# Five halves of expert weights loaded ahead of the overflow branch instead of ten, and the context's first split behind the copies of x

## The chip, the cores and the metric

The kernel runs on one core of a Trainium2 chip. The metric is the device time of one execution in microseconds (us). A core has a matrix engine (PE, with its weight loads as PEld), a vector engine (DVE), a scalar engine (ACT), a general engine (POOL) and an engine for synchronisation (SP), which in this kernel issues nearly all loads. Each engine runs its own list of instructions in order and waits for the others by semaphores.

## The reference, cut to what matters

The network has two blocks. The first mixes 256 tokens of width 1024, adds the result to x and then adds a mixture of experts: a router gives each token two of 32 experts, and each expert is a gated feed-forward network with a hidden width of 512. The second block needs keys and values of a 256-token context, which depend on the context alone and can be computed at any time.

```python
x = x + gt1 * mix
h2 = modulate(rms_norm(x, norm2_g[layer]), sh2, sc2)
x = x + gt2 * moe_ffn(h2.reshape(-1, D_MODEL), *moe_args).reshape(x.shape)
...
def moe_ffn(u, rg_w, rg_b, re_w, re_b, w1, w3, w2):
    ...
    yb = (jax.nn.silu(xblk @ w1[e]) * (xblk @ w3[e])) @ w2[e]
...
pc = modulate_2(rms_norm_2(cx, norm1_g[l]), csh1, csc1) @ w_in[l]
```

## The kernel before, in words

**Tiles.** Tokens are held as two halves of 128 partitions. All sums are in f32; a weight of a large product is split by `split_w` (L277) into a high part `wh` (ACT, L206) and a low part `wl` = `w` - `wh` (DVE, L209), and PE makes three products (`hh` by `wh`, `hl` by `wh`, `hh` by `wl`) where there was one. Splits come from a pool of 5 buffers. Weights come in halves of 128 x 2048 f32, 1 MB each, by `half` (L243) from the SP queue; in the expert stage ten buffers hold them.

**The place of the change.** At the end of the first mixer, `residual_part` adds the mixer's last product to x, in two halves of 512 columns. `route_part` (L911) transposes each finished piece of x on PE (products of `ident` by `x`), copies the result to `xT` on ACT and DVE by turns (L915, L916) and multiplies it by the router's weights on PE (into `pm_527`). `route_rows` (L921) scales these into `logit` on DVE. `route` (L929) is a chain of some 30 small DVE operations: the best group, the two best experts in it, `cnt`, then two kinds of small products on PE (`pm_591`), then `pos`, the place of each token in its expert's list, and `maxcnt` (L982), the largest number of tokens of one expert.

**Side steps.** `route_all` (L1077) also calls `side(SIDE0)` with `SIDE0` = 2: two steps of the context's computation, which is spread as filler over the expert stage, one step for each expert. The first two steps here are the products of the context with three chunks of `w_in_2`, of which the halves `w_603`, `w_604`, `w_615` and `w_616` matter here. `w_603` and `w_604` give 48 products of 128 x 256 each (`pf_605`, `pf_606`), `w_615` and `w_616` give 24 products of 128 x 512 each (`pf_617`, `pf_618`); the results go to `kvc`, which ACT writes to memory as `kv_d` (768 KB).

**The branch.** `overflow` (L1157) reads `maxcnt` into a register of every engine (L1161) and skips a block for lists of more than 32 tokens (L1162). With these inputs the block is never run. All engines pass the branch and wait for each other behind it. Behind it come the experts: `gather` (L1001) builds the one-hot matrix `oh` from `pos` on DVE, PE multiplies it with `xn` (16 products, `pm_718` and `pm_719`, recorded as 32), and ACT and DVE by turns scale the result into `xg`. `expert` then needs six halves of weights: two of e1, two of e3, two of e2. Expert 0 has `w_724` to `w_729`, expert 1 has `w_755` to `w_760`.

**What sets the order.** The program is written in the order of the computation, and the tile framework's scheduler then decides the order of instructions on each engine, by its own simulated times and by the dependences. `self.hold` is a list of pairs of instructions: `split_w` pops one pair and orders the high and the low split behind its two members (`behind`, a dependence of order). Expert 0's and 1's loads, which depend on no computation, were placed ahead of the branch by the scheduler as far as buffers allowed.

Of the kernel before, what the change touches and what calls it, by code (L numbers as in the profile page):

```python
# [20 lines left out]
P = 128  # L21
# [8 lines left out]
BGA = 1.34  # L30
NM = 0
XA, XB = 3, 5
SIDE, SIDE0 = 1.0, 2


C1 = dict(c=0, g1=16, g2=24, qk=32, hyu=40, cw=52, cb=88, skip=100, ffn=104)
# [5 lines left out]
class Lhs:  # L42
    def __init__(self, hi, lo):
        self.hi, self.lo = hi, lo
# [66 lines left out]
class Builder:  # L111
    def __init__(self, tc, a, ctx):
        self.tc, self.nc, self.a, self.ctx = tc, tc.nc, a, ctx
        E = ctx.enter_context
        self.p16 = E(tc.tile_pool(name="p16", bufs=5))
        self.p16x, self.nchunk = None, 0
        self.pspx, self.nsp = None, 0
        self.psp = E(tc.tile_pool(name="psp", bufs=5))
        self.p0 = E(tc.tile_pool(name="p0", bufs=1))
        self.psm = E(tc.tile_pool(name="psm", bufs=18))  # L120
        self.pr = E(tc.tile_pool(name="pr", bufs=4))
        self.pa = E(tc.tile_pool(name="pa", bufs=4, space=PSUM))
        self.pm = E(tc.tile_pool(name="pm", bufs=2, space=PSUM))
        self.pf = E(tc.tile_pool(name="pf", bufs=2, space=PSUM))
        self.n = 0
        self.p1 = None
        self.fill = False
        self.bg = None
        self.rot = 0
        self.flow = ""  # L130
        self.hold, self.gap = [], None
        self.early, self.s8 = (), None
        self.misc_pools, self.lin_misc = ["m"], False

# [87 lines left out]
        return self.nc.vector.scalar_tensor_tensor(out, a, s, b, op0=op0, op1=op1)  # L222

    def load(self, t, src):
        self.nc.sync.dma_start(t, src)

    def lsm(self, t, src):
        self.nc.gpsimd.dma_start(t, src)
# [14 lines left out]
    def half(self, src):  # L243
        self.nchunk += 1
        x = self.p16x and self.nchunk * self.nx % (5 + self.nx) < self.nx
        pool = self.p16x if x else self.p16
        t = pool.tile([P, 2048], F32, tag="T16", name=self.nm("w"))
        self.load(t, src)
        return t


# [659 lines left out]
    def route_part(self, x, xT, p, i):  # L911

        for k in range(4 * i, 4 * i + 4, 2):
            q = self.tr_pair(x, k)
            self.act(xT[:, k, :], q[:, 0, :])  # L915
            self.nc.vector.tensor_copy(xT[:, k + 1, :], q[:, 1, :])  # L916
            for kk in range(k, k + 2):
                for t in range(2):
                    self.mm(p[:, t], xT[:, kk, t * P:(t + 1) * P], self.router[0][:, kk, :], t == 0 and kk == 0, kk == 7)
# [81 lines left out]
    def gather(self, xn, A, B, e0, n):  # L1001

        oh = self.t2([P, 2, 8, 32], F32, "oh")[:, :, :n]
        es = slice(e0, e0 + n)
        for t in range(2):
            self.tt(oh[:, t], self.iota.unsqueeze(1).to_broadcast([P, n, 32]),
                    self.pos[:, t, es].unsqueeze(2).to_broadcast([P, n, 32]), ALU.is_equal)
        xg = self.t8([P, 8, 256], F32, "xg")
        w = 32 * n
        per = 512 // w  # L1010
        for d0 in range(0, 8, per):
            p = self.ps().rearrange("p (i s) -> p i s", s=w)
            for i, t in itertools.product(range(per), range(2)):
                d = d0 + i
                self.mm(p[:, i], xn[:, t, d * P:(d + 1) * P], oh[:, t].rearrange("p e c -> p (e c)"),
                        i == 0 and t == 0, t == 1)
            for i in range(per):
                d = d0 + i
                if i % 2 == 0:
                    self.act(xg[:, d, :w], p[:, i], AF.Identity, scale=A[:, d:d + 1], bias=B[:, d:d + 1])  # L1020
                else:
                    self.ts(xg[:, d, :w], p[:, i], A[:, d:d + 1], B[:, d:d + 1], ALU.mult, ALU.add)
        return oh, xg
# [53 lines left out]
    def route_all(self, x, side, more):  # L1077

        self.p_keep = self.p1
        xn = self.t8([P, 2, 1024], F32, "xn")  # L1080
        with self.tc.tile_pool(name="over", bufs=1) as self.p1:
            self.route()
            for t in range(2):
                self.ts(xn[:, t, :], x[:, t, :], self.r2[:, t:t + 1])
            side(SIDE0)
            for _ in range(NM):
                next(more)
            self.overflow(x, xn)
        return xn, self.A2, self.B2
# [872 lines left out]
def _tables():  # L1962
# [17 lines left out]
    def rope(half, nf):  # L1980
        inv = (f(10000.0) ** (-np.arange(nf, dtype=f) / f(nf))).astype(f)
        ang = np.zeros((2 * half, 256), f)
        rot = np.zeros((2 * half, 2 * half), f)
        for s, pos in ((0, r), (1, c)):
            for i in range(nf):
                a, b = s * half + i, s * half + nf + i
                ang[a] = ang[b] = pos * inv[i]
                rot[b, a] = -1.0
                rot[a, b] = 1.0
        return np.cos(ang), np.sin(ang), rot  # L1990
# [118 lines left out]
```

## Time and profile before

| what | value |
|---|---|
| median of 3 runs | 1779.25 us (1779.24 to 1780.82) |
| the profiled execution's own time | 1783.12 us |
| its span in the profile | 1781.4 us |
| mean granted clock of PE | 0.977 of full speed |
| PE busy | 1673.6 us, 94% of the span |
| DVE, ACT busy | 963.9 us (54%), 727.3 us (41%) |

The span is the profiled execution from its first to its last instruction. The profiled execution took 1783.12 us, 3.87 us more than the median. Times below, such as "at 448.1", are microseconds from the span's start.

### The profile page before, as it was taken

How to read it: one execution, taken by the hardware profiler on the slowest of the kernel's cores; microseconds unless marked ns; L12 is line 12 of the kernel's file. 1: busy time of each engine (PE TensorE's matmuls, PEld its weight loads, DVE VectorE, ACT ScalarE, POOL GpSimd, SP SyncE). 2: the span in 40 equal slices, each digit the busy share in tenths (PEclk: the TensorE clock that was granted, in tenths of full speed). 3: DMA queues.
4: the chain of work that ended last, by engine and by line, in shares of the span. 5: the costliest groups of instructions: out<-in, count | busy, mean ns of one | idle time of the engine just before them, and what ended most of it. 6: DMA issues, size and time to landing. Idle time of an engine off the chain costs nothing.

```text
span 1781.4 us, 31112 instructions
## 1 busy us (share of the span) xinstructions
PE 1673.6 (94%) x12928; PEld 1319.8 (74%) x12928; DVE 963.9 (54%) x1719; ACT 727.3 (41%) x1257; POOL 63.0 (4%) x104
## 2 busy tenths in 40 slices
PE   5999999999798889999999988999999999989998
PEld 1678766668565556777687667868999997689998
DVE  5626556466223445545454466685545466756555
ACT  2414433343223333333333236564444455645443
POOL 0000000000000000000000001010000000100000
PEclk9899999999899999999999999999999999989999
DMA  9654588977699999889999997634867746235551
GB/s 373 274 213 166 206 309 316 349 269 275 245 420 421 420 384 393 351 356 420 420 368 421 420 393 239 205 104 145 292 252 265 269 164 197 81 122 190 190 190 44
DMA packets 79059, 495.82 MB, mean 278 GB/s; under 512 B 8928, under 2 KB 15744, under 8 KB 22464
## 3 DMA queue, kind: packets, MB, share of 16 engines
q1 hardware_dynamic: 74496, 478.30, 69.9%
q0 software_dynamic: 3152, 10.47, 2.1%
q10 hardware_dynamic: 1264, 4.98, 0.7%
q8 instruction: 104, 1.70, 0.4%
q14 instruction: 43, 0.35, 0.1%
HBM read 486.91 MB, written 6.82 MB: 277 GB/s over the span
## 4 chain that ended last, share of the span: by engine, by line
PE 65%; DVE 4%; ACT 3%; issue 2%; DMA 1%; DVEq 0%; ACTq 0%
PE pf L200 24%; PE pm L200 19%; PE acc L200 11%; PE pa L200 5%; PE pj L200 2%; PE pm L203 1%; DMA w<-in_e 1%; PE pf L203 1%; PE pada L200 1%; DVE wl L209 1%; ACT e L206 0%; DVE sm L1337 0%; DMA w<-in_w_out 0%; ACT wh L206 0%; ACT eh L206 0%
## 5 line engine op out<-in xcount | busy, mean ns | idle before, releaser
L209 DVE TENSOR_TENSOR wl<-w,wh 128x1024 fp32r<-128x1024 f32 x346 | 422.2, 1224 | 399.1 <-PE pa L200 105.0
L206 ACT ACTIVATE wh<-w 128x1024 fp32r<-128x1024 f32 x346 | 362.5, 1057 | 406.2 <-PE pa L200 169.4
L200 PE MATMUL pf<-hh,wh 128*128 128x256 f32 x592 | 167.0, 284 | 3.6 <-ACT hh L206 2.3
L200 PE MATMUL pf<-hl,wh 128*128 128x256 f32 x592 | 165.5, 281 | 0.6 <-DVE hl L209 0.6
L200 PE MATMUL pf<-hh,wl 128*128 128x256 f32 x592 | 164.0, 282 | 1.5 <-DVE wl L209 1.5
L200 PE MATMUL acc<-hh,wh 128*128 128x256 f32 x512 | 143.5, 280 | 0.0
L200 PE MATMUL acc<-hl,wh 128*128 128x256 f32 x512 | 142.9, 279 | 0.0
L200 PE MATMUL acc<-hh,wl 128*128 128x256 f32 x512 | 142.8, 279 | 0.0
L200 PE MATMUL pm<-w,xg 128*32 128x256 f32 x2048 | 133.2, 392 | 2.5 <-DMA w<-in_e 1.2
L200 PEld LDWEIGHTS pf<-hh,wh 128*128 128x128 f32 x592 | 111.8, 189 | 8.6 <-issue 3.3
L200 PEld LDWEIGHTS pf<-hl,wh 128*128 128x128 f32 x592 | 111.8, 189 | 2.6 <-issue 1.2
L200 PEld LDWEIGHTS pf<-hh,wl 128*128 128x128 f32 x592 | 110.6, 189 | 3.4 <-DVE wl L209 2.5
L200 PEld LDWEIGHTS pm<-w,xg 128*32 128x32 f32 x2048 | 67.0, 112 | 52.3 <-issue 14.3
L200 PEld LDWEIGHTS acc<-hh,wh 128*128 128x128 f32 x512 | 96.4, 188 | 5.9 <-ACT wh L206 4.2
L200 PEld LDWEIGHTS acc<-hh,wl 128*128 128x128 f32 x512 | 96.7, 189 | 0.0
L200 PEld LDWEIGHTS acc<-hl,wh 128*128 128x128 f32 x512 | 96.4, 188 | 0.0
L200 PE MATMUL pada<-w,csil 128*32 128x512 f32 x576 | 84.5, 620 | 4.3 <-DMA w<-in_ada_w 4.3
L200 PE MATMUL pm<-w,ex 128*32 128x256 f32 x1024 | 62.1, 382 | 16.7 <-issue 15.5
L200 PE MATMUL pm<-hl,wh 128*128 128x256 f32 x256 | 71.7, 280 | 0.0
L200 PE MATMUL pm<-hh,wh 128*128 128x256 f32 x256 | 71.7, 280 | 0.0
L200 PE MATMUL pm<-hh,wl 128*128 128x256 f32 x256 | 71.4, 279 | 0.0
L200 PE MATMUL pf<-wl,hh 128*128 128x512 f32 x160 | 65.3, 408 | 0.0
(512 smaller groups left out, 3473.8 us busy)
## 6 DMA issues: line engine op xcount, KB each, us to landing
w<-in_e SPq DMA_DIRECT2D x192, 1024.0 KB, 12.4
w<-in_ff SPq DMA_DIRECT2D x96, 1024.0 KB, 5.0
w<-in_ada_w SPq DMA_DIRECT2D x72, 1024.0 KB, 7.0
w<-in_w_in SPq DMA_DIRECT2D x54, 1024.0 KB, 7.3
w<-in_w_out SPq DMA_DIRECT2D x16, 1024.0 KB, 7.1
w<-in_ret_w_o SPq DMA_DIRECT2D x4, 1024.0 KB, 5.3
w<-in_w_su SPq DMA_DIRECT2D x3, 1024.0 KB, 4.9
adab<-in_ada_b SPq DMA_DIRECT2D x9, 256.0 KB, 12.6
```

What stands on the lines that cost most here:

```text
L200: return self.nc.tensor.matmul(out, lhsT, rhs, start=start, stop=stop, skip_group_check=True)
L203: return self.nc.tensor.transpose(out, in_, self.ident)
L206: return self.nc.scalar.activation(out, in_, f, **k)
L209: return self.nc.vector.tensor_tensor(out, a, b, op=op)
```

## The change

The change has two parts. `gather` keeps the second of its first two `oh` operations as `self.gate`; from then on `half` counts its loads and gives numbers 6 to 15 a dependence on it, with a semaphore. The scheduler may thus put five halves (`w_724` to `w_728`) ahead of the branch and no more. And `route_all` fills `hold` with the last two copies into `xT`, so that the next `split_w`, which is that of the first half of `w_603`, is ordered behind them.

```diff
-SIDE, SIDE0 = 1.0, 2
+SIDE, SIDE0, EARLY = 1.0, 2, 5
...
+        self.gate, self.loads = None, 0
...
     def load(self, t, src):
-        self.nc.sync.dma_start(t, src)
+        return self.nc.sync.dma_start(t, src)
...
-        self.load(t, src)
+        i = self.load(t, src)
+        if self.gate:
+            self.loads += 1
+            if EARLY < self.loads <= EARLY + 10:
+                self.tc.add_manual_dep(i.ins, self.gate.ins.name, mybir.DependencyInfo(mybir.DependencyClass.Sync,
+                                       mybir.DependencyReason.DATA), reason="behind the branch")
         return t
...
-            self.act(xT[:, k, :], q[:, 0, :])
-            self.nc.vector.tensor_copy(xT[:, k + 1, :], q[:, 1, :])
+            self.moved = self.act(xT[:, k, :], q[:, 0, :]), self.nc.vector.tensor_copy(xT[:, k + 1, :], q[:, 1, :])
...
-            self.tt(oh[:, t], self.iota.unsqueeze(1).to_broadcast([P, n, 32]),
+            i = self.tt(oh[:, t], self.iota.unsqueeze(1).to_broadcast([P, n, 32]),
                     self.pos[:, t, es].unsqueeze(2).to_broadcast([P, n, 32]), ALU.is_equal)
+        self.gate = self.gate or i
...
             for t in range(2):
                 self.ts(xn[:, t, :], x[:, t, :], self.r2[:, t:t + 1])
+            self.hold = [self.moved]
             side(SIDE0)
```

Three engines' orders show it. First SP, whose instructions are the loads; `maxcnt` is its read of the register for the branch. Before, the last loads ahead of the branch:

```order
L225 DMA w_755_4072<-in_e1 128x2048
L225 DMA w_604_3283<-in_w_in_2 128x2048
L225 DMA w_616_3406<-in_w_in_2 128x2048
L225 DMA w_725_3938<-in_e3 128x2048
L225 DMA w_727_3942<-in_e3 128x2048
L225 DMA w_729_3946<-in_e2 128x2048
L225 DMA w_756_4074<-in_e3 128x2048
L225 DMA w_757_4076<-in_e1 128x2048
L225 DMA w_758_4078<-in_e3 128x2048
L1161 TENSOR_LOAD maxcnt_3251
```

And in the change, where line numbers are larger by 1 to 7:

```order
L226 DMA w_604_3283<-in_w_in_2 128x2048
L226 DMA w_616_3406<-in_w_in_2 128x2048
L226 DMA w_725_3938<-in_e3 128x2048
L226 DMA w_727_3942<-in_e3 128x2048
L1168 TENSOR_LOAD maxcnt_3251
...
L1169 UNCONDITIONAL_BRANCH
L226 DMA w_729_3946<-in_e2 128x2048
L226 DMA w_755_4072<-in_e1 128x2048
L226 DMA w_756_4074<-in_e3 128x2048
L226 DMA w_757_4076<-in_e1 128x2048
L226 DMA w_758_4078<-in_e3 128x2048
```

Five halves, `w_729` and `w_755` to `w_758`, moved from before the branch to right behind it.

Second DVE, around the chain of the router from `logit` on. Before, three low splits stand ahead of `logit` here (and those of `w_603` further up):

```order
L209 TENSOR_TENSOR wl_612_3344<-w_604_3283,wh_611_3343 128x1024
L916 COPY xT_526_2893<-pm_566_3124 128x256
L209 TENSOR_TENSOR wl_614_3372<-w_604_3283,wh_613_3371 128x1024
L209 TENSOR_TENSOR wl_620_3411<-w_615_3404,wh_619_3410 128x1024
L222 SCALAR_TENSOR_TENSOR logit_575_3157<-pm_527_2894,r2_567_3135,router_2879 128x36 x2
L933 TENSOR_REDUCE sm_577_3203<-logit_575_3157 128x2
...
L209 TENSOR_TENSOR pr_580_3211<-logit_575_3157,sm_578_3205 128x64
L209 TENSOR_TENSOR wl_622_3427<-w_615_3404,wh_621_3426 128x1024
L933 TENSOR_REDUCE sm_581_3213<-pr_580_3211 128x16
```

And in the change:

```order
L921 COPY xT_526_2893<-pm_566_3124 128x256
L210 TENSOR_TENSOR wl_608_3288<-w_603_3281,wh_607_3287 128x1024
L210 TENSOR_TENSOR wl_610_3316<-w_603_3281,wh_609_3315 128x1024
L223 SCALAR_TENSOR_TENSOR logit_575_3157<-pm_527_2894,r2_567_3135,router_2879 128x36 x2
L938 TENSOR_REDUCE sm_577_3203<-logit_575_3157 128x2
...
L210 TENSOR_TENSOR cnt_3235<-sm_578_3205,sm_589_3233 128x64
L210 TENSOR_TENSOR wl_614_3372<-w_604_3283,wh_613_3371 128x1024
L223 SCALAR_TENSOR_TENSOR pos_3246<-pm_591_3240,cnt_3235 128x64
```

The two low splits of `w_603` come behind the last copy into `xT`, `logit` comes right behind them, and the splits of `w_604` come within the chain. The low splits of `w_616` (`wl_624`, `wl_626`) stand behind the branch and behind `oh`.

Third PE, at the branch. Before, all products of `w_616` (splits `wh_623` to `wl_626`) and the first score product of the context, `pf_739`, precede the branch, and the gather follows it:

```order
L200 MATMUL pf_618_3409<-wh_625_3458,hh_505_2818 128x512
L200 MATMUL pf_618_3409<-wl_626_3459,hh_505_2818 128x512
L200 MATMUL pf_618_3409<-wh_625_3458,hl_506_2819 128x512
L200 MATMUL pf_739_4030<-kvc_495_2793,pad_601_3277 128x256
L1161 TENSOR_LOAD maxcnt_3251
...
L200 MATMUL pm_718_3899<-oh_716_3895,xn_576_3197 128x128 x7
L200 MATMUL pm_719_3912<-oh_716_3895,xn_576_3197 128x128 x7
```

And in the change:

```order
L201 MATMUL pf_618_3409<-wh_621_3426,hl_506_2819 128x512
L1168 TENSOR_LOAD maxcnt_3251
...
L201 MATMUL pf_617_3408<-wh_623_3442,hh_505_2818 128x512
L201 MATMUL pf_618_3409<-wh_623_3442,hh_505_2818 128x512
L201 MATMUL pm_718_3899<-oh_716_3895,xn_576_3197 128x128 x6
L201 MATMUL pf_617_3408<-wl_624_3443,hh_505_2818 128x512
...
L201 MATMUL pf_618_3409<-wh_625_3458,hl_506_2819 128x512
L201 MATMUL pm_718_3899<-oh_716_3895,xn_576_3197 128x128
L201 MATMUL pm_719_3912<-oh_716_3895,xn_576_3197 128x128 x8
L201 MATMUL pf_739_4030<-kvc_495_2793,pad_601_3277 128x256
```

All 24 products of `w_616` and `pf_739` moved behind the branch, where they stand among the products of the gather. Behind it on ACT are now also the high split `wh_625`, the four copies into `kvc`, which stand ahead of the first `xg`, and the write of `kv_d`. Ahead of the branch, PE has the router's transposes and products in one run and the products of `w_603` behind them, where before these began first and the router's stood among them. The scheduler's order also differs in details of the expert stage up to about a half of PE's list, and nowhere after that.

## Rows read from the trace of the kernel before

**Rows 1.** The page's busy time of each engine, and its chain that ended last.

```profile
PE 1673.6 (94%) x12928; PEld 1319.8 (74%) x12928; DVE 963.9 (54%) x1719; ACT 727.3 (41%) x1257; POOL 63.0 (4%) x104
...
PE 65%; DVE 4%; ACT 3%; issue 2%; DMA 1%; DVEq 0%; ACTq 0%
```

**Rows 2.** The chain of waits behind the branch: start us, us, what.

```profile
454.53 6.77 PE pm L200 x32
...
461.33 0.47 ACT xg L206
...
463.11 3.99 PE pm L200 x64
```

**Rows 3.** Instructions of the branch's two lines: ns min/median/max, first and last start.

```profile
L1161 SPq TENSOR_LOAD <-maxcnt x1: 469/469/469, 445.7 to 445.7; - x1
...
L1161 PEldq TENSOR_LOAD <-maxcnt x1: 489/489/489, 448.1 to 448.1; - x1
...
L1162 SPq COMPARE_BRANCH x1: 50/50/50, 446.6 to 446.6; - x1
L1162 PEldq COMPARE_BRANCH x1: 5212/5212/5212, 448.7 to 448.7; - x1
```

**Rows 4.** What SP waited for, 440 to 466 us: total, times, longest us.

```profile
SPq L225 <- PE pm L200: 12.9, 1, 12.9
...
SPq L1161 <- DVE maxcnt L982: 3.2, 1, 3.2
```

**Rows 5.** Timeline of PE ahead of the branch: start us, us, work, idle before it.

```profile
417.09 0.28 PE L200 MATMUL pf<-hh,wh 128*128 128x256 f32 x1
...
426.80 0.38 PE L200 MATMUL pf<-hh,wh 128*128 128x256 f32 x1 [1.33 <-ACT wh L206]
...
434.87 0.50 PE L200 MATMUL pf<-wh,hh 128*128 128x512 f32 x1 [0.99 <-ACT pad L206]
```

**Rows 6.** Timeline of DVE ahead of the branch.

```profile
419.19 0.68 DVE L209 TENSOR_TENSOR x<-x,a 128x512 f32<-128x512 f32 x1
...
426.78 1.23 DVE L209 TENSOR_TENSOR wl<-w,wh 128x1024 fp32r<-128x1024 f32 x1 [1.60 <-ACT wh L206]
...
431.73 0.41 DVE L222 SCALAR_TENSOR_TENSOR logit<-pm,r,router 128x36 f32<-128x36 f32 x2
...
439.79 0.23 DVE L209 TENSOR_TENSOR cnt<-sm,sm 128x64 f32<-128x64 f32 x1
...
445.49 0.15 DVE L982 CAST maxcnt<-sm 128x1 int32<-128x1 f32 x1
```

**Rows 7.** Timeline of ACT ahead of the branch.

```profile
446.79 1.35 ACT L206 ACTIVATE kvc<-pf 128x256 f32<-128x256 f32 x4 [0.57 <-PE pf L200]
```

**Rows 8.** Stretches: us, busy us (instructions) of PE, PEld, DVE, ACT, POOL, PEclk, DMA, GB/s.

```profile
424.00:434.00 10.00, 8.39 (x70) 7.83 (x68) 6.61 (x15) 5.00 (x7) 0.99 (x2) 1.00 1.01 419
...
450.47:454.50 4.03, 0.00 (x0) 0.00 (x0) 0.40 (x2) 0.00 (x0) 0.00 (x0) 0.50 0.13 46
454.50:460.70 6.20, 6.17 (x29) 6.20 (x30) 1.34 (x5) 0.91 (x2) 0.50 (x1) 0.50 0.01 3
...
703.06:706.47 3.41, 1.73 (x33) 0.82 (x25) 3.31 (x12) 2.03 (x4) 0.79 (x1) 1.00 0.95 348
706.47:713.30 6.83, 6.83 (x52) 3.80 (x52) 4.90 (x14) 2.53 (x6) 0.00 (x0) 0.50 0.78 277
```

**Rows 9.** DMA by queue 448 to 450 and 450 to 452 us, and an issue.

```profile
q10 hardware_dynamic: 71, 0.44, 52.8%
...
q8 instruction: 1, 0.02, 3.0%
...
kv_d<-kvc ACTq DMA_DIRECT2D x1, 768.0 KB, 3.9
```

**Rows 10.** Timeline of PE, the second gather.

```profile
505.87 3.62 PE L200 MATMUL pm<-oh,xn 128*128 128x128 f32 x30
```

**Rows 11.** The chain of waits, 640 to 760 us.

```profile
656.38 17.48 DMA w<-in_e
```

## The prediction

> **What bounds the kernel now.** I read the page first. PE is busy 94% of the span, and the chain that ended last runs on PE for 65% of it, with small shares of DVE and ACT and 1% of waits for loads [rows 1]. So a change gains where it closes a hole of PE, and loses where it opens one. The change works between 417 and 467 us; the next view is therefore the chain of waits there. It enters behind the branch: a gather on PE of 6.77 us from 454.53, then `xg` (0.47 us on ACT), then expert 0's products at 463.11 [rows 2]. From there to the end the work follows from expert 0 step by step, mostly on PE, so I take it that a shift of 463.11 arrives at the end undiminished, and make my sum to that time.
>
> Next come the branch's own instructions. SP reads the register at 445.7 and its compare takes 0.05 us. PE arrives last but for DVE and ACT, at 448.1, and its compare takes 5.21 us [rows 3]; the gather begins at 454.53, so the branch costs PE 454.53 - 448.1 = 6.4 us. What does SP wait for there? It waits 3.2 us for `maxcnt` and only behind the branch 12.9 us for buffers, which expert 0's products free [rows 4]. The branch thus waits for PE and the router's chain and not for the expert weights ahead of it. That is the first finding against the edit's plain reading.
>
> Last I read the stretches. PE had nothing to do from its read of the register at 448.1 on; from 450.47 to 460.70 it was granted half of its clock (1.2 of 2.4 GHz), and 6.2 us of that were work [rows 3, 8]. The gather shows the price: 32 recorded products in 6.77 us, against 30 in 3.62 us in the second gather [rows 2, 10].
>
> **Part one, the loads.** Five halves leave the queue ahead of the branch. A half is 128 x 2048 x 4 bytes = 1.05 MB; at the 419 GB/s of a stretch with busy DMA engines it takes 2.5 us [rows 8]. PE's wait of 1.33 us at 426.80, ahead of `w_604`'s first product, has a part that goes away, since `w_755` no longer stands ahead of `w_604` [rows 5]; the second part of the change moves that product anyway. Behind the branch five halves need 5 x 2.5 = 12.4 us. Issued at about 449.3, as `oh` is done, they have landed by about 463.4 (with 1.7 us for a start). Expert 0's first products need `w_724` to `w_727`, which are early; `w_729` is needed with the second half of its output product, about 4.9 us after 463.11, and expert 1's halves later. Behind the waiting loads SP has only later halves, and those waited for expert 0 to free a buffer anyway (12.9 us [rows 4]); POOL has no part in it. Cost: nothing. The cover is the gather and `xg`; without it, two halves' time, 5 us.
>
> **Part two, the split behind the copies.** Before, the products of `w_603` start at 417.09 and fill PE while x gets its last sum (419.19, 0.68 us) [rows 5, 6]. Now they wait. PE's last mixer product ends at 417.25; then the sum ends at 419.9, two rounds of transposes, copies and router products follow, which I put at 2.4 us each (an estimate; they were spread among other work before); the last copy ends at about 424.8, `wl_608` (1.23 us [rows 6]) is there at 426.0. In between PE has the router's products and the first four high products, about 3.7 us, so a hole of about 5 us opens. In return the chain runs early: `logit` moves from 431.73 to about 427.2, `cnt` from 439.79 to 432.9 and `maxcnt` from 445.49 to about 435, since fewer splits stand ahead of them on DVE [rows 6].
>
> PE up to the branch, then: 48 products of `w_603` at 0.117 us (the spacing of the rows behind 417.09) bring it to 431.2; 48 of `w_604` with the small `cnt` products and a wait for `pos` bring it to 438.0; 1.0 us for `pad` as before at 434.87 [rows 5]; 24 of `w_615` at 0.234 us bring it to 444.6. It arrives 3.5 us before 448.1, but the 24 products of `w_616` and `pf_739` (24 x 0.234 + 0.3 = 5.9 us) are still to do. So PE's work stands 2.4 us later.
>
> **The branch.** What will it cost? The nearest rows differ widely: PE's own 6.4 us above, and about 2 us if PE passed as the other engines did (SP from its read at 445.7 to its compare's end at 446.7 is 1 us [rows 3]; I add 1 us for the others' signals). While PE's compare ran, the write of `kv_d` (768 KB, 3.9 us) had half of the DMA engines' time, and one packet of an instruction queue came only at its end [rows 9]. In the change this write is behind the branch. I take 1.8 us off: 4.6 us, with 6.4 and 2.0 as the ends, nearer to the first because it is PE's own row. PE resumes at 444.6 + 4.6 = 449.2.
>
> The Trainium skill ("Runtime: NRT & Kernel Launch", "Instruction fetch mechanics") says that a taken branch whose target is outside the fetched window must wait for a fetch by DMA; the 5.21 us of PE's compare beside SP's 0.05 agree. But its page "DMA: Bandwidth & Descriptors", "Queues, rings and completion order", says that a DMA engine takes turns between queues packet by packet, so that a write in another queue would hardly delay a fetch; by that rule nothing comes off, and the sum below would be +3.8 instead of +2.0.
>
> **Behind the branch.** To the last context product PE now has 24 products of `w_616` (5.6 us) and seven of the gather's 16 at 0.23 us (3.62 us / 30 x 2 records [rows 10]), together 7.2 us at full clock. The clock falls as before, and I keep 6.2 us at half [rows 8], which costs 3.1 us more: 449.2 + 7.2 + 3.1 = 459.4, rounded over the parts. (If the shorter pause spares half of it, 1.6 less; 8 us at half, 0.9 more.) Then, what is not beside PE's work: four copies into `kvc`, which ACT must finish ahead of the first `xg` (1.35 us [rows 7]), eight `xg` by turns on ACT and DVE of 0.45 us (3.6) [rows 2], and two more ACT operations ahead of expert 0, `sc` and one of a context step (0.8, an estimate from the same row): 5.75 us. Before, the first `xg` could start while the gather ran. Expert 0 starts at 465.1 instead of 463.11.
>
> **Sum.** +2.0 us. The profiled execution is 3.9 us above the median of the runs shown; I add the 2.0 to the median: 1779.25 + 2.0 = about 1781. A change of 0.2% is 3.56 us, about what a measurement of this kernel can tell from no change.
>
> **Rivals.**
> - *The branch costs PE 6.4 us as now.* For it: this is the only row of a PE branch here; the write of `kv_d` took only half of the engines. Against: the packet that came late. Expert 0 starts 1.8 us later: +3.8, 1783.
> - *A cheap branch (the other side: faster).* If PE's fetch is delayed by the write alone, or the target is fetched while PE still multiplies, the branch costs 2.0, and the clock hardly falls because PE paused so briefly: 2.0 - 2.6 - 3.1 = -3.7, about 1775.5. It decides if PE's compare is below 1 us. Against it: no PE branch here shows it.
> - *The clock falls in the new hole (slower).* In the stretch 703.06 to 706.47 PE was busy for half of the time, and the 6.83 us behind it ran at half clock [rows 8]. The hole from 417.3 to 426 has PE busy for less than half. If the clock falls, 3.4 us at half cost 1.7 and 6.8 cost 3.4. With 3.4, and the branch between the two prices (+0.9): 1779.25 + 2.0 + 3.4 + 0.9 = 1785.5. The point of decision is the granted clock behind 420.
> - *The new order of the expert stage.* The scheduler moved rows as far as half way through PE's list. A late load there has its price in the chain: 17.48 us at 656 are a load of expert weights that PE waits on [rows 11]. A quarter of that, some 4 us, I leave open either way: about 1775 or 1785 with the +2.0.
> - *The change doesn't do what it says.* If the branch waits for no loads [rows 4], five loads fewer ahead of it change nothing, and only the second part works. That is already in my sum.
>
> **How the numbers follow.** Chances: forecast 0.40; branch at its old price 0.15 (half of it past 0.2%); cheap branch 0.17 (0.14 past 0.2%); the fallen clock 0.10; the expert stage 0.18, half on each side. Faster: 0.14 + 0.09 = 0.23. Slower: 0.08 + 0.10 + 0.09 = 0.27. The rest, 0.50, is within 0.2%. The likeliest case alone reaches from 1778 (clock spared by half, fetch sooner) to 1784 (old price). The range for 8 in 10 reaches below to the cheap branch with a microsecond more, 1774.5, and above to the fallen clock, 1786.5.
>
> **What would show it.** Right: SP's read of the register near 436 to 445, not held by any load; PE's last product ahead of the branch near 444.6 and its compare about 3.4 us; PE idle some 5 us between 417.3 and 426; the first product of expert 0 near 465. Wrong: a compare of under 1 us on PE, a granted clock of half ahead of 440, `w_729` or an expert 1 half as the releaser of a PE wait, or an end that moved by other than the start of expert 0, which would put the cause in the expert stage.

## The result, and the profile after

| | before | changed kernel |
|---|---|---|
| median | 1780.03 us (4 runs, 1779.24 to 1782.19) | 1795.89 us (4 runs, 1795.17 to 1801.24) |
| ratio | | 1.0085 (95% interval 1.0067 to 1.0102) |
| profiled execution | 1783.12 us, span 1781.4 | 1795.42 us, span 1793.7 |

The change makes the kernel some 16 us slower, outside the predicted range of 1774.5 to 1786.5. The page says little: PE's share is 94% as before and the chain's shares have hardly moved [rows 1]. PE's busy time has grown by 10.2 us with the same 12928 products, so the loss does not show as idle time alone.

```profile
PE 1683.8 (94%) x12928; PEld 1321.3 (74%) x12928; DVE 965.1 (54%) x1719; ACT 727.9 (41%) x1257; POOL 61.6 (3%) x104
...
PE 64%; DVE 4%; ACT 3%; DMA 2%; issue 2%; DVEq 0%; ACTq 0%; SPq 0%
```

So I follow the stages. First the branch (the same view as [rows 3], in the changed kernel: ns min/median/max, first and last start):

```profile
L1168 SPq TENSOR_LOAD <-maxcnt x1: 474/474/474, 436.3 to 436.3; - x1
...
L1168 PEldq TENSOR_LOAD <-maxcnt x1: 487/487/487, 442.3 to 442.3; - x1
...
L1169 PEldq COMPARE_BRANCH  x1: 3309/3309/3309, 442.9 to 442.9; - x1
```

SP reads the register 9.4 us earlier, PE 5.8 us earlier, and PE's compare takes 3.31 us instead of 5.21. What SP waits for, as in [rows 4], here from 415 us on:

```profile
SPq L1168 <- DVE maxcnt L987: 13.7, 1, 13.7
...
SPq L226 <- DVE oh L210: 6.4, 1, 6.4
```

SP's read waits for `maxcnt` alone, longer since no load keeps SP busy, and its next load waits 6.4 us for the gate. What does the branch cost PE? The timeline of PE's first product behind it, before and after (the idle time stands in brackets):

```profile
454.53 6.76 PE L200 MATMUL pm<-oh,xn 128*128 128x128 f32 x32 [6.32 <-DVE oh L209]
```

```profile
446.33 0.70 PE L201 MATMUL pf<-wh,hh 128*128 128x512 f32 x2 [0.26 <-PEq L1169]
```

PE's sequencer reads the register while products that it has issued are still to run: 15 of them start behind the read at 442.3, the last at 445.69. So the compare runs beside work, and PE stands idle for 0.26 us. Before, no product was left behind the read, and it stood idle for 6.32 us. Then the chain behind the branch, as in [rows 2] (start us, us, what), and the stretches, as in [rows 8] (us, busy us of PE, PEld, DVE, ACT, POOL, granted clock, DMA share, GB/s):

```profile
446.33 0.70 PE pf L201 x2
447.04 1.34 PE pm L201 x12
...
453.76 2.01 PE pm L201 x18
455.77 0.45 PE pf L201 x2
...
458.84 3.66 PE pm L201 x64
```

```profile
417.20:422.00 4.80, 3.34 (x24) 2.74 (x24) 4.38 (x18) 1.78 (x6) 1.07 (x2) 1.00 0.19 31
422.00:428.80 6.80, 6.28 (x27) 6.02 (x28) 6.36 (x19) 3.34 (x4) 0.99 (x2) 0.50 0.98 405
428.80:441.60 12.80, 11.80 (x95) 11.37 (x95) 8.93 (x33) 6.54 (x11) 0.00 (x0) 1.00 0.38 157
...
446.30:460.00 13.70, 12.62 (x92) 10.29 (x96) 5.86 (x13) 4.79 (x15) 1.17 (x1) 1.00 0.88 316
```

Expert 0 starts at 458.84, which is 4.3 us *earlier* than before [rows 2]. The clock did fall, but in the new hole ahead of the branch (422.0 to 428.8), and behind the branch it stayed full. So the loss of 12.3 us in the span lies behind expert 0, where the change edits no instruction and only its late halves could still be felt. Where? The copy `eh` marks every expert (32 of them: first and last start in one row). Before and after:

```profile
L206 ACT ACTIVATE eh<-pm x32: 363/384/387, 467.1 to 1067.1; 128x256 f32<-128x256 f32 x32
```

```profile
L207 ACT ACTIVATE eh<-pm x32: 365/385/387, 462.5 to 1077.6; 128x256 f32<-128x256 f32 x32
```

Expert 0 is 4.6 us early, expert 31 10.5 us late. What PE waited for between 465 and 1090 us, before and after (engine, line, releaser: total us, times, longest):

```profile
PE pm L200 <- issue: 15.5, 14, 1.8
...
PE pm L203 <- ACT eh L206: 7.6, 16, 0.6
```

```profile
PE pm L201 <- issue: 21.9, 18, 2.8
PE pm L204 <- ACT eh L207: 10.8, 20, 1.3
```

Eighteen pauses instead of fourteen. An expert has two: after its first products PE needs `eh` from ACT before it can transpose it, and after the transposes it needs two small steps of ACT and DVE before the output products. One such expert (number 19, counted from 0), in the chain of the kernel before and of the changed kernel:

```profile
818.91 3.93 PE pm L200 x68
822.84 3.00 PE pf L200 x12
825.84 0.22 PE pm L203 x2
826.05 2.82 PE pf L200 x12
...
828.88 1.93 PE pm L200 x32
```

```profile
819.22 0.39 ACT eh L207
...
819.66 0.45 PE pm L204 x2
820.11 1.04 issue
821.15 1.93 PE pm L201 x32
823.09 3.00 PE pf L201 x12
```

Before, twelve products of the context (`pf`) stand in each pause. Now the expert's three steps stand one behind the other, PE waits through ACT's copy and the 1.04 us, and twelve of the context's products come afterwards. The printed orders show the same: 14 pauses of each kind without a product in them before, 18 of each now.

To place the loss I matched PE's instructions of two traces one by one by the printed orders and summed, by stretch of the kernel before, how much longer each took up to the next one's start:

```
stretch of before, us     417-465   465-790   790-1090
changed kernel               -4.8      +0.3      +16.6
run one                      +0.2      -5.3       +2.3
run two                      -0.2       0.0      +17.1
second split held            -3.9      -5.0       +3.2
```

(The other rows are runs told below. Single profiles differ from each other by some us, since stretches at half clock lie elsewhere in each.)

How much of the 16.6 us are the pauses? From start to start, between 790 and 1090 us, the step from an expert's first products to its transposes took 8.1 us in 9 pauses before and 12.6 us in 13 now, and the step from the transposes to the output products 10.6 us in 8 and 16.2 us in 12. These are 10 us for four experts, 2.5 us each. Some 2 or 3 us are the clock: the kernel before has no half clock in this stretch, the changed kernel 6.8 us, and run one, with the old order and 7.3 us at half clock, is 2.3 us longer there. The rest are smaller waits, some longer and some shorter than before.

### The profile page after: what moved, and what is told of

Its sections match the earlier page's. It is cut to its first block, busy times and chain, and to the rows that moved or that the text cites. A ratio compares the mean times of both kernels' runs of the same rounds, so it can differ in the third digit from the quotient of the medians.

```text
span 1793.7 us, 31114 instructions
## 1 busy us (share of the span) xinstructions
PE 1683.8 (94%) x12928; PEld 1321.3 (74%) x12928; DVE 965.1 (54%) x1719; ACT 727.9 (41%) x1257; POOL 61.6 (3%) x104
## 4 chain that ended last, share of the span: by engine, by line
PE 64%; DVE 4%; ACT 3%; DMA 2%; issue 2%; DVEq 0%; ACTq 0%; SPq 0%
PE pf L201 24%; PE pm L201 19%; PE acc L201 11%; PE pa L201 5%; PE pj L201 2%; PE pm L204 1%; DMA w<-in_w_in 1%; DVE wl L210 1%; PE pf L204 1%; DMA w<-in_e 1%; PE pada L201 1%; ACT wh L207 1%; ACT e L207 0%; ACT eh L207 0%; DVE sm L1344 0%
## 5 line engine op out<-in xcount | busy, mean ns | idle before, releaser
L201 PE MATMUL pm<-w,xg 128*32 128x256 f32 x2048 | 136.9, 389 | 1.3 <-DMA w<-in_e 0.7
L201 PEld LDWEIGHTS pm<-w,ex 128*32 128x32 f32 x1024 | 34.1, 112 | 46.3 <-issue 29.8
## 6 DMA issues: line engine op xcount, KB each, us to landing
adab<-in_ada_b SPq DMA_DIRECT2D x9, 256.0 KB, 12.6
```

What stands on the lines that cost most here:

```text
L201: return self.nc.tensor.matmul(out, lhsT, rhs, start=start, stop=stop, skip_group_check=True)
```

## The experiments

Theory A: the head of the change, up to expert 0, is no loss; the loss is the scheduler's other order of the expert stage, which leaves more pauses unfilled. Theory B: the five halves loaded late starve a stage that moves weights at 420 GB/s. The tool for it is a table that pins an order. It holds, for each of the five engines, the numbers of the instructions in the order wanted (the loads' order on SP too), and adds a dependence of order, without a semaphore, from each to the one behind it:

```diff
+def pin_order(tc, nc):
+    for ids in ORDER.values():
+        for a, b in zip(ids[:-1], ids[1:]):
+            tc.add_manual_dep(nc.find_inst_by_name(f"I-{b}"), f"I-{a}", mybir.DependencyInfo(mybir.DependencyClass.NoSync,
+                              mybir.DependencyReason.DATA), reason="order")
```

"Old tail" below is the order of the kernel before from expert 0's own products to the end of the context's steps, "new tail" that of the changed kernel.

**Run one: both parts, old tail.** Edit: the changed kernel plus the table.

> The changed kernel with both parts, but from expert 0's own products on every engine keeps the order of the kernel before (a table of order, no data dependence). Theory A (the expert stage's other order lost the time, the head gained): expert 0 starts near 459 as in the changed kernel, the lead of about 4.4 us lasts to the end, 1775.5 us, ratio 0.9975. Theory B (the five halves loaded late leave the DMA engines idle ahead of the branch, and the stage behind, which moves weights at 420 GB/s, pays for it): as the changed kernel, near 1796 us, ratio 1.009.

1780.74 us, ratio 1.0001 (0.9992 to 1.0010). The loss is gone, so the order made it. But the lead that theory A promised is not there either:

```profile
420.60:430.80 10.20, 9.26 (x42) 8.47 (x41) 8.83 (x35) 3.60 (x5) 2.05 (x4) 0.50 0.86 330
...
461.50:468.40 6.90, 6.90 (x61) 6.33 (x64) 1.42 (x5) 1.36 (x5) 0.00 (x0) 0.51 0.78 294
```

Ahead of the branch the order is that of the changed kernel on every engine, yet 10.2 us were at half clock instead of 6.8, and 6.9 us more in expert 0. Behind the branch the table did more than I meant. DVE's four `xg` stand behind a step of the context (`a`), as in the kernel before, where the changed kernel has three of them ahead of it. DVE in the changed kernel, then in run one:

```profile
454.84 0.41 DVE L220 TENSOR_SCALAR xg<-pm,A,adac 128x128 f32<-128x128 f32 x1 [5.50 <-ACT xg L207]
...
457.50 0.35 DVE L219 TENSOR_SCALAR a<-a,sm 128x256 f32<-128x256 f32 x1
```

```profile
459.73 0.35 DVE L219 TENSOR_SCALAR a<-a,sm 128x256 f32<-128x256 f32 x1
460.00 0.41 DVE L220 TENSOR_SCALAR xg<-pm,A,adac 128x128 f32<-128x128 f32 x1
```

From PE's first product behind the branch to expert 0's first product it takes 14.1 us (448.60 to 462.73) instead of 12.4 (446.33 to 458.77). Run one's `eh` came at 469.3, not 462.5. Of these 6.8 us, 2.3 were there at the branch, 1.7 go with the table's order of `xg`, and 2.8 with the half clock in expert 0. So the head's 4.3 us belong in part to one execution, and in part the table took them away.

**Run two: neither part, new tail.** Edit: the kernel before plus the table.

> The kernel before, neither part of the change, but from expert 0's own products on every engine has the order of the changed kernel. Theory A: the old head (expert 0 at 463) and the whole loss of the stage, about 16.6 us: 1796.5 us, ratio 1.0093. Theory B: the order is not to blame, near 1780 us, ratio 1.000 to 1.002.

1799.43 us, ratio 1.0107 (1.0091 to 1.0122): the whole loss and some 3 us more than I expected, with nothing of the change in the program but its order. PE's waits repeat those of the changed kernel:

```profile
PE pm L200 <- issue: 21.8, 18, 2.8
```

**Run three: part one alone, old tail.**

```diff
-            self.hold = [self.moved]
```

> Part one alone (five halves behind the branch), the order of the kernel before everywhere else. Theory A: the loads are hidden behind the gather, expert 0 starts near 463, 1779 to 1781 us, ratio 1.000. Theory B: five halves are late in a stage bound by its loads, up to 5 x 2.5 = 12.4 us: 1785 to 1792 us, ratio 1.003 to 1.007.

1784.97 us, ratio 1.0022 (1.0011 to 1.0034): some 4 us slower. Theory B holds at a third of its size. In this profile PE waits for a late half once between 490 and 530 us, at expert 3; the kernel before has no such wait there:

```profile
PE pm L201 <- DMA w<-in_e: 1.5, 1, 1.5
```

**Run four: part two alone, old tail.**

```diff
-        self.gate = self.gate or i
```

> Part two alone (the first split behind the copies of x), ten halves ahead of the branch as before, the order of the kernel before from expert 0 on. Theory A: the head's gain comes from this part, expert 0 starts near 459, 1775.5 us, ratio 0.9975, no more than 1 us from the run with both parts. Theory B: faster than the run with both parts by up to 12 us, near 1775 us while that one stays near 1796.

1781.31 us, ratio 1.0005 (0.9994 to 1.0016). Neither theory's 1775. The order is run one's on every engine, with its late `xg`, and again there is a stretch at half clock, 418.8 to 429.0. I take it that these two cost the gain of the earlier branch; run seven tries the clock. Run one, which has part one as well, is no slower (1780.74 us): with this head part one has no cost that shows.

```profile
418.80:429.00 10.20, 9.25 (x43) 8.43 (x42) 8.75 (x34) 3.60 (x5) 2.05 (x4) 0.51 0.87 329
```

**Runs five and six: the new order in one stretch only.** Edit: the kernel before plus the table, with the new order for the instructions of experts 17 to 21, or 23 to 27.

> The kernel before; only in the stretch that ran from 787 to 877 us before (experts 17 to 21) every engine has the order of the changed kernel. Theory A (each pause of an expert that loses its filling costs PE its length, and the loss stays to the end): run two lost 2.6 and 3.9 us of PE there and won 0.8, so expert 22 about 6 us late and 1786 us, ratio 1.0033. Theory C (the stage is bound by its loads, a loss of PE in one place is made up while PE waits for loads elsewhere): expert 22 late, but under 2 us left at the end, ratio below 1.0012.

> The kernel before; only in the stretch that ran from 890 to 1010 us before (experts 23 to 27) every engine has the order of the changed kernel. Theory A: run two lost 2.0, 2.5 and 3.5 us of PE there, so expert 29 about 8 us late and 1788 us, ratio 1.0045. Theory C: under 2 us left at the end.

1.0033 (1.0019 to 1.0047) and 1.0040 (1.0025 to 1.0054). Each loses what the same stretch of the kernel before lost in run two (matched as above: 6.7 against 6.6 us, 7.6 against 7.8), and the loss stays to the end; theory C falls. The unfilled pauses of the two kinds, 2 and 1 more in run five, 2 and 2 more in run six, are 3.1 and 4.6 us of it from start to start; the rest are the smaller waits. Together the two runs make 13 of run two's 19 us.

**Run seven: hold the second split, not the first.** Ten halves early, old tail:

```diff
-            self.hold = [self.moved]
+            self.hold = [(), self.moved]
...
-        self.gate = self.gate or i
```

> Part two changed: not the first but the second split of the first context half is ordered behind the copies of x, so that PE has 24 products for the hole ahead of the router; ten halves ahead of the branch as before; the order of the kernel before from expert 0 on. If the clock fell because the hole left PE idle: no stretch at half clock between 417 and 440, PE at the branch near 441, expert 0 at 456 to 460 instead of 463, 1774 to 1777 us, ratio 0.9965 to 0.998. If the clock falls anyway or the router's chain, later by a low split of 1.2 us, holds the branch: as the run with part two alone, 1780 us.

1776.32 us, ratio 0.9969 (0.9957 to 0.9981), 0.3% faster than the kernel before. PE has 24 products while x gets its last sum, and the clock stays full ahead of the branch; expert 0 starts at 458.1:

```profile
417.20:428.00 10.80, 9.39 (x76) 8.64 (x75) 8.75 (x27) 5.19 (x10) 2.05 (x4) 1.00 0.56 210
428.00:441.00 13.00, 12.53 (x89) 11.45 (x88) 10.45 (x40) 6.63 (x12) 0.00 (x0) 1.00 1.02 421
```

**Run eight: fill two pauses.** Edit: run seven's table with nine products moved into the pauses of each of two experts.

> As the run with the second split held, and for two experts (22 and 28) nine of the 24 context products that stood ahead of or among the expert's first products moved into its two pauses (three ahead of its transposes, six behind them); on DVE the expert's two steps moved ahead of the context's. 12 and 12 unfilled pauses instead of 14 and 14. Theory A: 2 x (0.6 + 1.3) = 3.8 us less, 1772.5 us, ratio 0.9948. Theory C (the loads bind here): no gain, ratio 0.997.

1774.05 us, ratio 0.9954 (0.9941 to 0.9968), the best here. Expert 22 in the chain of run seven, then of run eight:

```profile
877.63 0.39 ACT eh L207
...
878.06 0.45 PE pm L204 x2
878.52 1.05 issue
879.56 1.97 PE pm L201 x32
```

```profile
873.04 1.85 PE pm L201 x28
874.89 0.89 PE pf L201 x3
875.78 0.23 PE pm L204 x2
```

The copy and the 1.05 us are covered. Matched as above, PE gains 1.5 us in each of the two stretches, 3.0 in all, where I expected 3.8. PE's waits of the two kinds fall by as much: for `eh` from 7.6 us, 16 times, to 6.7, 14 times, and behind the transposes from 15.5 us, 14 times, to 13.4, 12 times. The two medians differ by 2.3 us, and the two intervals overlap, so the gain rests on the profile more than on the times.

**Run nine: run seven with part one.**

```diff
+        self.gate = self.gate or i
```

> As the run with the second split held, and with part one of the change (five halves behind the branch); the order of the kernel before from expert 0 on. If late loads cost by themselves: about 3 us more, as the run with part one alone showed (expert 3 and 5 wait for a half), 1779 us, ratio 0.9985 to 0.999. If the earlier branch hides them: 1776 us, ratio 0.997.

1778.85 us, ratio 0.9990 (0.9978 to 1.0001), 2.5 us behind run seven: part one seems to cost here too, though the intervals just overlap. The profile (1776.64 us, no longer than run seven's 1776.95) shows where. Expert 0 comes 1.1 us earlier than in run seven, and from expert 2 to 3 and from 4 to 5 PE loses 0.9 and 0.8 us against it, the same two places at which run three loses 2.1 and 1.1 us against the kernel before. At expert 3 PE waits 0.30 us for a half of weights (1.48 us in run three, 0.73 in the changed kernel). Run one came to this expert 5.5 us later than the changed kernel and shows no such wait.

**Run ten: run seven without the table.**

> As the run with the second split held, but without the table of order: the scheduler decides the expert stage, with 17 and 18 unfilled pauses where the kernel before has 14 and 14 and the changed kernel 18 and 18. Theory A: loses like the changed kernel, some 15 us more than with the table, 1789 to 1793 us, ratio 1.005 to 1.007. Rival: the order does not matter for this head, 1776 us.

1787.9 us, ratio 1.0037 (1.0024 to 1.0051): 12 us more than with the table, for 17 and 18 unfilled pauses; I had expected 1789 to 1793. Its head is even better: expert 0's first product comes at 456.3, in run seven at 458.1; here three of DVE's four `xg` stand ahead of the context's step, as in the changed kernel. The good head is lost to the order that the scheduler lands on.

## Why the prediction was wrong, step by step

*What failed first: "I take it that a shift of 463.11 arrives at the end undiminished".* It does if the order behind it stays. It did not: 16.6 us were lost from 790 us on. I had this as a rival, the new order of the expert stage, and gave it 4 us either way from the price of one late load [rows 11], and a chance of 0.18. The price was of the wrong kind and too small. Part of it could have been read off beforehand: the printed orders of the two kernels show how many experts have no product in their pauses, 14 and 18, and the trace of before has the idle time of such a pause (15.5 us in 14 waits behind the transposes, 7.6 us in 16 for `eh`). Four experts more are 6.3 us by that, an estimate, on the right side but under half of the loss: from start to start an unfilled expert costs 2.5 us, and smaller waits in the same stretches add to it. Runs two, one, five and six show that the order alone makes the loss. How it divides between the pauses and the rest is read from profiles; only run eight moves little besides the products of two pauses.

*The range followed from that step.* It reached to 1786.5 for a fallen clock, and it let a reordering in with 4 us only.

*The head's sum, +2.0.* Its parts, against the changed kernel's profile:

- The router's earlier chain: right. `maxcnt` was read at 436.3, I had said 435; SP's read waited for no load. The hole of PE was smaller: 2.0 us idle between 417.2 and 428.8 (from the rows of stretches above), not 5. PE's last product ahead of the branch started at 445.7, I had said 444.6.
- The branch at 4.6 us: wrong, the second step that failed. I let PE resume 4.6 us after its last product. The compare took 3.31 us where I had 3.4, but it ran beside 15 products already issued, and PE stood idle for 0.26 us: it resumed at 446.33, not at 449.2. That is the way of the cheap branch, a rival with a chance of 0.17 ("the target is fetched while PE still multiplies"); its sign, a compare below 1 us, was the wrong one, since the compare is the sequencer's time and not PE's. The guess about `kv_d`'s write holds for the compare's length: over all kernels run, it took 5.19 to 5.25 us in the five that issue the write ahead of it, and 3.31 to 4.59 us in the seven that issue it behind. The Trainium skill ("DMA: Bandwidth & Descriptors", "Queues, rings and completion order") says that a DMA engine takes turns between queues packet by packet. I had drawn from it that a fetch would hardly wait for another queue's write, which gave +3.8; these lengths go against that use of it.
- Half clock behind the branch, 3.1 us: wrong here. The clock fell in the hole ahead of it, which was a rival of its own (0.10), and stayed full behind, where PE had paused for 0.26 us only. In run one it fell in the hole and again in expert 0, so one profile does not fix this term.
- Up to the last context product: 9.9 us (446.33 to 456.21) against 10.2, by luck. The 3.1 us of clock were not in it, but all 16 products of the gather were, where I had counted seven.
- The copies ahead of expert 0, 5.75 us: wrong. From PE's last product at 456.21 to expert 0 at 458.84 it took 2.6 us; the `xg` ran beside a step of the context.
- "Cost: nothing" for the loads: right for this head with the old order, wrong with the others. Run one is no slower than run four; runs three and nine put it at 2.5 to 4 us. `w_729` did land in time for expert 0, but the five halves landed at 453.6 to 466.1, not by 463.4; no run shows the 1.7 us that I allowed for a start. The halves behind them follow each other by 2.5 us, about 420 GB/s, so what leaves the queue late there stays late; I asked only about the first user of each half, and the wait came at expert 3.

So expert 0 stood at 458.84 in this profile, 6.3 us ahead of the 465.1 of my sum: 2.9 by the branch, 0.3 by the products, 3.1 by the copies. With the order behind it held still the change is worth nothing in time, 1.0001 in run one, which is the forecast's "within 0.2%". That agreement is luck: the terms of the head were wrong one by one, and in run one the table's late `xg` and the clock took back what the branch had saved.

## What to carry to other kernels

If a scheduler orders the program, an edit in one place is an edit everywhere: compare the orders over the whole program, count in each the dependent steps that stand back to back, and price them by a pause of the trace. To test an idea by itself, pin the order of the rest. When a stage is moved, look not only for the hole's length but for whether PE has work in it: the second split held instead of the first (run seven against run four) left no half clock ahead of the branch instead of 10.2 us, and saved some 5 us. And a branch costs PE little while products that it has issued still run.

## What the runs showed of the hardware

Between 400 and 1700 us the granted clock fell in stretches of 3.4, 6.8 or 10.2 us, always to half, and not at the same places in two kernels that have the same order up to the branch: 422.0 to 428.8 in the changed kernel, 420.6 to 430.8 in run one. With the hole partly filled it was none in runs seven and eight up to the branch, and 3.4 us in runs nine and ten. The head of the kernel before had none there in three profiles and 3.4 us in two (runs three and six). So one profile of such a kernel can be off by about 5 us in a place that the edit does not touch (10.2 us at half clock, an estimate), and the head's worth had to be read from the ratios of many runs.

PE's sequencer read the register and compared while products that it had issued were still to run. In the seven kernels with 15 products still to start behind the read, PE stood idle for 0.26 to 2.04 us at the branch; in the five with none, for 6.3 to 6.4 us.

That a write of 768 KB by another queue stretches a compare of PE from 3.3 to 5.2 us I had guessed, not expected to see so steadily. The packets in the traces bear it out: in the five kernels with the write ahead, a packet of 16 KB of an instruction queue (q8) starts 2.9 us behind the start of the compare, within 0.02 us of the end of the write's last packet; in the changed kernel and runs one and nine, with neither this write nor loads beside the compare, it starts 1.0 us behind it. The write was not moved by itself in any run. What sets the compare between 3.31 and 4.59 us was not tried. In runs four, seven and eight, with 3.85 to 4.59 us, expert weights were still landing during the compare; but so they were in run ten, with 3.33.
